# Down projection of a hybrid decoder step: three groups of contraction tiles, two of them in seven products for eight

## Chip, core and metric

The kernel runs on one core of a Trainium2 chip. The metric is the device time of one execution in microseconds (us). TensorE (PE) multiplies, VectorE (DVE), ScalarE (ACT) and GpSimd (POOL) do the elementwise work, and SyncE (SP) issues nearly all transfers, in order.

## What is computed

One layer of a decoder trunk, for 512 prompt tokens and 64 sampled tokens (NT = 576 columns), width 1024, everything in float32. Only the feed-forward part and what follows it matter here (D_FF = 2816 = 22 tiles of 128, D_MODEL = 8 tiles of 128):

```python
hf = rmsnorm(h, w['norm_ffn'])
h = h + (jax.nn.silu(hf @ w['w_gate']) * (hf @ w['w_up'])) @ w['w_down']
gate = jax.nn.sigmoid(rmsnorm(h, w['norm_ple']) @ w['w_ple_gate'])
h = h + gate * (p.astype(h.dtype) @ w['w_ple_proj'])
return rmsnorm(h, norm_final)
```

## The kernel before

**Layout.** Activations are held transposed: a tile is 128 features by 576 tokens. A matmul takes a 128x128 block of weights and 288 columns, one of two column halves, `N1` and `N2`. To keep float32 precision, every operand is split into a high part and a remainder (`split` L185, `wsplit` L197): ACT copies the high part, DVE or POOL subtracts it from the source to get the low part, and three matmuls (high by high, high by low, low by high) make one product. Which of DVE and POOL subtracts alternates from split to split (`flip`, L192 and L204) unless the call names one.

**Plain products.** `linear` (L225) loads weights in blocks of four contraction tiles (`wload`, a 128x512 block of 256 KB, three `raw` buffers), splits each, and issues 3 x 4 x 2 matmuls per block.

**The seven-product form.** `gate_pair` (L1411) makes two output tiles of the gate projection. It treats the 8 contraction tiles as two halves of four, the two output tiles as the rows, and the two column halves as the columns of a 2x2 block product, which it does in seven products instead of eight (Winograd's form of Strassen's scheme). It loads four weight blocks a11, a21, a22 (three buffers, tag `raw2`) and a12 (tag `raw`, shared with `wload`), and forms s1 = a21 + a22, s2 = s1 - a11, s4 = a12 - s2 on DVE and a11 - a21 on POOL (L1416 to L1419). Each of the seven `product` calls (L1399) splits its weight combination (tags `wh`, `wl`, three buffers each; three of the low parts are named for POOL, four for DVE) and issues 12 matmuls. `kept` (L1406) copies four of the sums out of PSUM on ACT, POOL adds three of them (L1429, L1434, L1435), and DVE finishes the two outputs and scales them by `rs`, the row norms. The right-hand combinations of the normed input, T1 to T4, are built once, at L1377 to L1387.

**The feed-forward stage.** Pair 0 is done plainly (L1355). For pairs 1 to 10, `gate_pair` is followed by two plain up projections (`linear(XF, ...)`, L1460, 96 matmuls), their product with silu(gate), and `inner` (L1350), which splits the two finished inner tiles into `ah`, `al` (low part on POOL). `down` (L1446) is called after pair 5 with 12 inner tiles and after pair 10 with 10: for each of 8 output tiles it runs `linear`, scales the sum by `rs` on DVE (L1451) and adds it to the residual tile `hs[c]` on POOL (L1452). The second call also runs `after` (L1299) for each output tile: ACT makes the high part and a square, DVE the low part (L1303), POOL adds up the squares (L1310). The gate of the per-layer embedding (L1498 on) takes these as its operands; the weights of its second and third output tile wait for the root of the norm (L1499), its first does not.

**Order of the work.** A planner orders the instructions of each engine when the program is built: in program order, with later instructions drawn forward where its timing model sees an engine idle. Each engine's order is then fixed, and its instructions wait for their inputs in that order. PSUM is used in four tiles of two banks (`lin_bank`, L103).

Of the kernel before, what the change touches and what calls it, by code (L numbers as in the profile page):

```python
# [16 lines left out]
P = 128  # L17
D = 1024
NT = 576
# [1 line left out]
HALF = 288  # L21
KT = D // P
NFF = 22
NSPLIT = 6
C_DECAY = math.exp(-0.5)
EPS = 1e-6
GN_EPS = 64e-5
# [48 lines left out]
def hybrid_step(ctx, tc, A):  # L76
# [1271 lines left out]
    AF2 = []  # L1348

    def inner(s_):  # L1350

# [3 lines left out]
    for f in range(2):  # L1355
        ps = lin_ps()
        linear(XF, ps, WLAST)
        if f == 0:
            up = lin_ps()
            linear(XF, up, WLAST)  # L1360
            rs = rstd_of(st)
        s_ = ft("sg")
        V.tensor_tensor(s_[:], ps, rs[:], ALU.mult)
        act(s_[:], s_[:], AF.Silu)
        if f:
            up = lin_ps()
# [29 lines left out]
        wat[0] += P * 512  # L1396
        return t

    def product(ps, w, n, first, eng):  # L1399
        hi, lo = split(w[:], cm, ("wh", "wl"), [P, 512], lo_eng=eng, bufs=3)  # L1400
        for p, q in WLAST:
            for k in range(4):
                T.matmul(ps, (hi, lo)[p][:, k * P:(k + 1) * P], OPS[n][k][q], start=first and p == q == k == 0,  # L1403
                         stop=p == 1 and k == 3, skip_group_check=True)

    def kept(ps):  # L1406
# [1 line left out]
        act(t[:], ps)  # L1408
        return t

    def gate_pair():  # L1411

        a11, a21, a22 = (block() for _ in range(3))
        a12 = block(wp, "raw")
        s1, s2, s4 = (cm.tile([P, 512], F32, tag="sw", name=nm("sw"), bufs=3) for _ in range(3))
        V.tensor_tensor(s1[:], a21[:], a22[:], ALU.add)  # L1416
        V.tensor_tensor(s2[:], s1[:], a11[:], ALU.subtract)
        G.tensor_tensor(a21[:], a11[:], a21[:], ALU.subtract)
# [4 lines left out]
        product(a, a11, "B11", True, V)  # L1423
        p1 = kept(a)
        product(b, s2, "T2", True, G)
        p6 = kept(b)
        product(c, s1, "T1", True, V)
        p5 = kept(c)
        G.tensor_tensor(p6[:], p6[:], p1[:], ALU.add)  # L1429
        product(a, a12, "B21", False, G)  # L1430
        V.tensor_tensor(sa[:, N1], a, rs[:, N1], ALU.mult)
        product(b, a21, "T3", False, V)
# [3 lines left out]
        product(c, s4, "B22", False, G)  # L1436
        V.tensor_tensor(sa[:, N2], c, p6[:], ALU.add)
        V.tensor_tensor(sa[:, N2], sa[:, N2], rs[:, N2], ALU.mult)
        product(b, a22, "T4", False, V)
        V.tensor_tensor(sb[:, N1], b, p1[:], ALU.add)  # L1440
        V.tensor_tensor(sb[:], sb[:], rs[:], ALU.mult)
        for s_ in (sa, sb):
            act(s_[:], s_[:], AF.Silu)
        return sa, sb

    def down(last):  # L1446
        for c in range(8):
            ps = lin_ps()
            linear(AF2, ps, WLAST)
            t = ft("dn")  # L1450
            V.tensor_tensor(t[:], ps, rs[:], ALU.mult)  # L1451
            G.tensor_tensor(hs[c][:], hs[c][:], t[:], ALU.add)  # L1452
            if last:
                after(c, hs[c], "norm_ple", pools[-1], "f", 9, st)
        AF2.clear()

    for p in range(1, NFF // 2):
        for s_ in gate_pair():
            up = lin_ps()
            linear(XF, up, WLAST)  # L1460
            V.tensor_tensor(s_[:], up, s_[:], ALU.mult)
            inner(s_)
# [72 lines left out]
def pack(inp):  # L1535
# [79 lines left out]
    for c in range(0, NFF, 2):  # L1615
# [7 lines left out]
        if c // 2 in (NSPLIT - 1, NFF // 2 - 1):  # L1623
            k0 = 0 if c // 2 == NSPLIT - 1 else 2 * NSPLIT
            for m in range(8):
                put_tile(wd, k0, c + 2 - k0, m)
    for c in range(8):
        put_tile(wpg, 0, 8, c)
    out["wts"] = np.concatenate(blocks)
# [43 lines left out]
```

## Time and profile before

| what | value |
|---|---|
| median of 3 runs | 1347.17 us (1346.14 to 1347.79) |
| span of the profiled execution, first to last instruction | 1349.0 us; its own device time is not listed beside the span, so the span stands for it |
| PE busy | 1246.8 us (92% of the span), 10525 matmuls |
| DVE, ACT, POOL busy | 826.0, 618.9, 625.6 us |
| transfers | 135.58 MB, mean 100 GB/s |
| feed-forward stage | about 862 to 1280 us of the span |

In the profile, "busy" is the time in which an engine has an instruction under way. Matmuls are pipelined, so the mean length of one (about 295 ns) is more than the distance from one to the next. A row such as `wl<-sw,wh` names what is written, then what is read. Times on the left of the timeline are microseconds from the start of the span.

### The profile page before, as it was taken

The page shows a single profiled execution, that of the slowest core. Times are in us where ns is not written, and L with a number is a line of the kernel's source. Part 1 is how long each engine was busy: PE and PEld are TensorE (multiplying, and loading weights), DVE is VectorE, ACT ScalarE, POOL GpSimd, SP SyncE. Part 2 cuts the span into 40 slices and gives each one's busy share as a digit, 9 for nine tenths or more (in the row PEclk, how much of TensorE's full clock was granted, in tenths as well). Part 3 has the DMA queues.
Part 4 walks back from the last instruction along what each step waited for, and adds up shares of the span by engine and source line. Part 5 has one row for each costly group of instructions (what it writes and reads, how often), then busy time and mean ns, then how long its engine had stood idle before and what let it go on. Part 6 is the DMA issues. An engine that isn't in the chain of part 4 may idle for free.

```text
span 1349.0 us, 26596 instructions
## 1 busy us (share of the span) xinstructions
PE 1246.8 (92%) x10525; PEld 1150.7 (85%) x10525; DVE 826.0 (61%) x1443; ACT 618.9 (46%) x1256; POOL 625.6 (46%) x597
## 2 busy tenths in 40 slices
PE   6897999999989978899999969989999999999997
PEld 6787897889868957788779859889999999999997
DVE  6648666887687785943466667886553135443454
ACT  6565436534654463343434364464442124433363
POOL 5425413642355154122456645565654336654642
PEclk9897799899979978889989989998999999999998
DMA  5322242234232412262454542222323222314322
GB/s 164 125 68 66 77 117 63 85 103 116 75 99 78 109 41 80 94 214 83 157 176 131 179 125 72 73 93 88 92 88 87 79 86 82 93 59 149 96 89 71
DMA packets 94461, 135.58 MB, mean 100 GB/s; under 512 B 34705, under 2 KB 39057, under 8 KB 94337
## 3 DMA queue, kind: packets, MB, share of 16 engines
q1 hardware_dynamic: 93760, 133.36, 32.4%
q8 instruction: 83, 1.36, 0.4%
q10 hardware_dynamic: 576, 0.52, 0.1%
q14 instruction: 42, 0.34, 0.1%
HBM read 106.10 MB, written 27.75 MB: 99 GB/s over the span
## 4 chain that ended last, share of the span: by engine, by line
PE 63%; DVE 14%; ACT 4%; issue 4%; DMA 3%; POOL 3%; DVEq 0%; SPq 0%; ACTq 0%; POOLq 0%
PE lin L234 21%; PE lin L1403 8%; PE lin L223 6%; PE lin L221 6%; PE lin L222 6%; DVE h L395 2%; PE lin L1508 1%; PE lin L1509 1%; PE lin L1510 1%; DVE tmp L674 1%; DVE wlo L206 1%; DVE Tt L676 1%; PE lin L613 1%; PE cx L797 1%; DVE suv L831 1%
## 5 line engine op out<-in xcount | busy, mean ns | idle before, releaser
L206 POOL TENSOR_TENSOR wlo<-raw,whi 128x512 fp32r<-128x512 f32 (+1 forms) x108 | 146.4, 1356 | 352.5 <-ACT whi L93 269.5
L93 ACT ACTIVATE whi<-raw 128x512 fp32r<-128x512 f32 (+1 forms) x232 | 143.3, 618 | 259.1 <-PE lin L234 126.4
L221 PE MATMUL lin<-xhi,whi 128*128 128x288 f32 (+1 forms) x784 | 243.3, 311 | 2.5 <-ACT whi L93 2.2
L223 PE MATMUL lin<-xhi,wlo 128*128 128x288 f32 (+1 forms) x784 | 241.5, 308 | 2.3 <-POOL wlo L206 2.3
L222 PE MATMUL lin<-xlo,whi 128*128 128x288 f32 (+1 forms) x784 | 241.5, 308 | 0.3 <-POOL xlo L194 0.3
L206 DVE TENSOR_TENSOR wlo<-raw,whi 128x512 fp32r<-128x512 f32 (+1 forms) x124 | 100.9, 814 | 103.2 <-PE lin L234 60.4
L221 PEld LDWEIGHTS lin<-xhi,whi 128*128 128x128 f32 (+1 forms) x784 | 151.0, 193 | 9.3 <-ACT whi L93 2.6
L223 PEld LDWEIGHTS lin<-xhi,wlo 128*128 128x128 f32 (+1 forms) x784 | 150.7, 192 | 6.2 <-POOL wlo L206 2.8
L222 PEld LDWEIGHTS lin<-xlo,whi 128*128 128x128 f32 (+1 forms) x784 | 150.8, 192 | 4.8 <-issue 1.2
L234 PE MATMUL lin<-xhi,whi 128*128 128x288 f32 x384 | 62.3, 297 | 3.2 <-ACT xhi L93 3.0
L234 PE MATMUL lin<-xlo,whi 128*128 128x288 f32 x384 | 60.8, 298 | 0.0
L234 PE MATMUL lin<-xhi,wlo 128*128 128x288 f32 x384 | 59.3, 297 | 0.0
L234 PEld LDWEIGHTS lin<-xhi,whi 128*128 128x128 f32 x384 | 54.6, 189 | 3.8 <-ACT xhi L93 1.7
L234 PEld LDWEIGHTS lin<-xlo,whi 128*128 128x128 f32 x384 | 54.8, 191 | 0.0
L234 PE MATMUL lin<-ah,wlo 128*128 128x288 f32 x352 | 54.7, 296 | 0.0
L234 PE MATMUL lin<-al,whi 128*128 128x288 f32 x352 | 54.7, 296 | 0.0
L234 PE MATMUL lin<-ah,whi 128*128 128x288 f32 x352 | 54.7, 296 | 0.0
L234 PEld LDWEIGHTS lin<-xhi,wlo 128*128 128x128 f32 x384 | 54.3, 191 | 0.0
L1403 PE MATMUL lin<-T,wh 128*128 128x288 f32 x320 | 50.1, 296 | 4.5 <-DVE T L194 2.8
L674 DVE TENSOR_TENSOR tmp<-L,Tt 72x30 f32<-72x30 f32 (+14 forms) x120 | 49.2, 410 | 3.2
L234 PEld LDWEIGHTS lin<-ah,whi 128*128 128x128 f32 x352 | 49.6, 189 | 0.0
L234 PEld LDWEIGHTS lin<-ah,wlo 128*128 128x128 f32 x352 | 49.6, 189 | 0.0
(425 smaller groups left out, 3197.8 us busy)
## 6 DMA issues: line engine op xcount, KB each, us to landing
raw<-wts SPq DMA_DIRECT2D x271, 256.0 KB, 2.6
S<-s_wkv SPq DMA_DIRECT2D x8, 512.0 KB, 5.1
hd<-s_ssm SPq DMA_DIRECT2D x8, 512.0 KB, 4.5
o_ssm_s<-hd SPq DMA_DIRECT2D x8, 512.0 KB, 2.9
xbc_d<-E SPq DMA_DIRECT2D x12, 288.0 KB, 2.1
x<-xT SPq DMA_DIRECT2D x8, 288.0 KB
gate_d<-g SPq DMA_DIRECT2D x8, 288.0 KB, 2.5
bv_d<-rw SPq DMA_DIRECT2D x8, 288.0 KB
```

Source lines behind the costliest of these rows:

```text
L93: return S.activation(out, in_, func, bias=bias, scale=scale)
L206: eng.tensor_tensor(lo[:, 0:n], raw[:, 0:n], hi[:, 0:n].bitcast(F32), ALU.subtract)
L221: T.matmul(ps[:, a:b], whi, xhi[:, a:b], start=first, stop=False)
L222: T.matmul(ps[:, a:b], whi, xlo[:, a:b], start=False, stop=False)
L223: T.matmul(ps[:, a:b], wlo, xhi[:, a:b], start=False, stop=last)
L234: T.matmul(ps[:, a:e], (hi, lo)[p][:, i * P:(i + 1) * P], xs[k + i][q][:, a:e], start=n == k + i == 0, stop=n == 2 and k + i == nk - 1, sk ...
L395: V.scalar_tensor_tensor(h[:], E[:, i:i + 600], w(i), h[:], ALU.mult, ALU.add)
L613: T.matmul(ps[:, c:c + 128].rearrange("p (a t) -> p a t", a=2), s.BK[jj][H[e], g].rearrange("p a t -> p (a t)"), s.G[H[e], g, jj, :, e], s ...
L674: V.tensor_tensor(o, L[:, jx:jx + 1, jx + 1:32].to_broadcast([NB, jx, n]), Tt[:, 0:jx, jx:jx + 1].to_broadcast([NB, jx, n]), ALU.mult)
L676: V.tensor_tensor(Tt[:, 0:jx, jx + 1:32], Tt[:, 0:jx, jx + 1:32], o, ALU.subtract)
L797: T.matmul(uw[H[e], jj, :], TT[H[e], g, jj, :], xs[H[e], jj, :], start=True, stop=True)
L1403: T.matmul(ps, (hi, lo)[p][:, k * P:(k + 1) * P], OPS[n][k][q], start=first and p == q == k == 0, stop=p == 1 and k == 3, skip_group_check ...
```

## The change

The 22 inner tiles are cut into three groups: pairs 0 to 3, pairs 4 to 7 and pairs 8 to 10 (`DOWNS = (4, 8)`). The first two groups of 8 inner tiles go through the seven-product form, for two output tiles at a time; the last group of 6 stays plain.

- `gate_pair`'s body becomes `seven(ops, r)`, with the operands and an optional scale as arguments. Without a scale, ACT copies the first quarter of the output out of PSUM and the two DVE multiplications by `rs` fall away.
- `operands(sa, sb)` replaces `inner` for pairs 0 to 7: four subtractions over half the columns (three on DVE, one on POOL) build the right-hand combinations, and four splits (one of 288 columns, three of 576) replace two. The split of B11 lies in buffers of tag `hx`, four of them, which take the place of the residual tiles 4 to 7.
- `down_pairs(d)` runs `seven` four times, for output tiles 0-1 to 6-7, and stores each of the eight sums, unscaled, to DRAM (`acc_d`).
- The residual tiles `hs[4]` to `hs[7]` are stored to DRAM when they are complete (`h_d`) and loaded again after the last pair.
- The last group: for each output tile two stored sums are loaded and added on POOL, DVE adds the plain product of the last 6 inner tiles and multiplies by `rs`, POOL adds the residual, then `after` as before. The pool of the late stage has 12 instead of 9 working tiles.
- The host packs the weights of the down projection in the new order.

```diff
-NSPLIT = 6
+DOWNS = (4, 8)
...
+    h_d, acc_d = dram("h", 4), [dram(f"acc{i}", 8) for i in range(2)]
...
     def residual(c, ps, src):
-        h = hp.tile([P, NT], F32, tag="h", name=nm("h"))
+        h = hp.tile([P, NT], F32, tag="hx" if c > 3 else "h", name=nm("h"), bufs=4)
...
         after(c, hs[c], "norm_ffn", me, "xs", 8, st)
+        if c > 3:
+            nc.sync.dma_start(h_d[c - 4][:], hs[c][:])
...
-        return pools[-1].tile([P, NT], F32, tag="f", name=nm(name), bufs=9 if len(pools) > 1 else 6)
+        return pools[-1].tile([P, NT], F32, tag="f", name=nm(name), bufs=12 if len(pools) > 1 else 6)
...
-    def product(ps, w, n, first, eng):
+    def product(ps, w, x, first, eng):
...
-                T.matmul(ps, (hi, lo)[p][:, k * P:(k + 1) * P], OPS[n][k][q], start=first and p == q == k == 0,
+                T.matmul(ps, (hi, lo)[p][:, k * P:(k + 1) * P], x[k][q], start=first and p == q == k == 0,
...
-    def gate_pair():
+    def seven(ops, r=None):
...
-        V.tensor_tensor(sa[:, N1], a, rs[:, N1], ALU.mult)
+        if r is None:
+            act(sa[:, N1], a)
+        else:
+            V.tensor_tensor(sa[:, N1], a, r[:, N1], ALU.mult)
...
+    def operands(sa, sb):
+
+        i = len(DOPS.setdefault("B11", []))
+        t, u = ft("t12"), ft("t34")
+        V.tensor_tensor(t[:, N1], sa[:, N2], sa[:, N1], ALU.subtract)
+        G.tensor_tensor(u[:, N1], sb[:, N2], sa[:, N2], ALU.subtract)
+        V.tensor_tensor(t[:, N2], sb[:, N2], t[:, N1], ALU.subtract)
+        V.tensor_tensor(u[:, N2], sb[:, N1], t[:, N2], ALU.subtract)
+        b = hp.tile([P, 2, HALF], F32R, tag="hx", name=nm("b11"), bufs=4)
+        hi, lo = split(sa[:, N1], None, None, None, hi=b[:, 0], lo=b[:, 1])
+        DOPS["B11"].append((hi, lo))
+        for n, (x, names) in enumerate(((sb, ("B21", "B22")), (t, ("T1", "T2")), (u, ("T3", "T4")))):
+            f = 3 * i + n
+            hl = split(x[:], fp, (f"ah{f}", f"al{f}"), [P, NT])
+            for c, name in zip((N1, N2), names):
+                DOPS.setdefault(name, []).append(tuple(y[:, c] for y in hl))
+
+    def down_pairs(d):
+        for c in range(0, 8, 2):
+            for i, t in enumerate(seven(DOPS)):
+                nc.sync.dma_start(acc_d[d][c + i][:], t[:])
+        DOPS.clear()
+
+    operands(*held)
     for p in range(1, NFF // 2):
-        for s_ in gate_pair():
+        pair_ = gate_pair()
+        for s_ in pair_:
             up = lin_ps()
             linear(XF, up, WLAST)
             V.tensor_tensor(s_[:], up, s_[:], ALU.mult)
-            inner(s_)
-        if p == NSPLIT - 1:
-            down(False)
+            if p >= DOWNS[-1]:
+                inner(s_)
+        if p < DOWNS[-1]:
+            operands(*pair_)
+        if p + 1 in DOWNS:
+            down_pairs(DOWNS.index(p + 1))
+    for c in range(4, 8):
+        hs[c] = hp.tile([P, NT], F32, tag="hx", name=nm("h"), bufs=4)
+        nc.sync.dma_start(hs[c][:], h_d[c - 4][:])
     cm_.close()
     pools.append(ctx.enter_context(tc.tile_pool(name="f2", bufs=1, side="right", reuse_waits="tile")))
     st = {"x": []}
-    down(True)
+    for c in range(8):
+        old = [ft("acc") for _ in acc_d]
+        for t, src in zip(old, acc_d):
+            nc.sync.dma_start(t[:], src[c][:])
+        G.tensor_tensor(old[0][:], old[0][:], old[1][:], ALU.add)
+        ps = lin_ps()
+        linear(AF2, ps, WLAST)
+        t = old[1]
+        V.tensor_tensor(t[:], ps, old[0][:], ALU.add)
+        V.tensor_tensor(t[:], t[:], rs[:], ALU.mult)
+        G.tensor_tensor(hs[c][:], hs[c][:], t[:], ALU.add)
+        after(c, hs[c], "norm_ple", pools[-1], "f", 12, st)
```

More of the change, by code (lines that the diff above doesn't have):

```diff
@@ L1344, in ft @@
     def ft(name):
[L1345 removed]
+        return pools[-1].tile([P, NT], F32, tag="f", name=nm(name), bufs=12 if len(pools) > 1 else 6)
     XF = st["x"]
[L1348 removed]
+    AF2, held, DOPS = [], [], {}
     def inner(s_):
@@ L1368, in hybrid_step @@
         V.tensor_tensor(s_[:], up, s_[:], ALU.mult)
-        inner(s_)
+        held.append(s_)
     cm_ = ExitStack()
@@ L1435, in gate_pair @@
         G.tensor_tensor(sb[:, N2], p67[:], p5[:], ALU.add)
-        product(c, s4, "B22", False, G)
+        product(c, s4, ops["B22"], False, G)
         V.tensor_tensor(sa[:, N2], c, p6[:], ALU.add)
-        V.tensor_tensor(sa[:, N2], sa[:, N2], rs[:, N2], ALU.mult)
-        product(b, a22, "T4", False, V)
+        if r is not None:
+            V.tensor_tensor(sa[:, N2], sa[:, N2], r[:, N2], ALU.mult)
+        product(b, a22, ops["T4"], False, V)
         V.tensor_tensor(sb[:, N1], b, p1[:], ALU.add)
-        V.tensor_tensor(sb[:], sb[:], rs[:], ALU.mult)
+        if r is not None:
+            V.tensor_tensor(sb[:], sb[:], r[:], ALU.mult)
+        return sa, sb
+    def gate_pair():
+        sa, sb = seven(OPS, rs)
         for s_ in (sa, sb):
@@ L1444, in gate_pair @@
         return sa, sb
[L1446 to L1455, printed above, removed]
+    def operands(sa, sb):
[19 more added lines that the diff above has]
+    operands(*held)
     for p in range(1, NFF // 2):
-        for s_ in gate_pair():
+        pair_ = gate_pair()
+        for s_ in pair_:
             up = lin_ps()
@@ L1622, in pack @@
             put_tile(wu, 0, 8, c + i)
[L1623 to L1626, printed above, removed]
+        if c // 2 + 1 in DOWNS:
+            lo_, hi_ = (list(range(c - 6 + i, c + 2, 2)) for i in range(2))
+            for m in range(0, 8, 2):
+                for ks, i in ((lo_, 0), (lo_, 1), (hi_, 1), (hi_, 0)):
+                    put(wd, ks, m + i)
+    for m in range(8):
+        put_tile(wd, 2 * DOWNS[-1], NFF - 2 * DOWNS[-1], m)
     for c in range(8):
```

11 lines of the change are left out of this document (5 added, 6 removed).

## The prediction

> **What bounds the kernel now.** I read the page first (busy shares, then the chain that ended last), then the feed-forward stage by windows, then the rows of the engines beside PE.
>
> ```profile
> span 1349.0 us, 26596 instructions
> PE 63%; DVE 14%; ACT 4%; issue 4%; DMA 3%; POOL 3%; DVEq 0%; SPq 0%; ACTq 0%; POOLq 0%
> L234 PE MATMUL lin<-ah,wlo 128*128 128x288 f32 x352 | 54.7, 296 | 0.0
> raw<-wts SPq DMA_DIRECT2D x271, 256.0 KB, 2.6
> ```
>
> PE is 63% of the chain. The third row is one of the three forms of the down projection: 3 x 352 = 1056 matmuls. The windows show the stage that the change touches: PE, PEld, DVE, ACT and POOL busy, then granted clock, DMA share and GB/s.
>
> ```profile
> 886.00:911.00 25.00, 20.74 (x153) 19.98 (x151) 24.41 (x30) 18.23 (x37) 19.51 (x16) 0.99 0.22 68
> ...
> 1020.00:1096.00 76.00, 76.00 (x572) 76.00 (x571) 15.97 (x21) 15.83 (x26) 29.67 (x21) 1.00 0.28 80
> 1101.74:1197.30 95.56, 95.56 (x723) 95.56 (x722) 53.07 (x64) 42.36 (x76) 58.39 (x44) 1.00 0.30 86
> 1217.00:1280.00 63.00, 63.00 (x474) 63.00 (x474) 21.82 (x28) 23.41 (x39) 35.61 (x26) 1.00 0.37 115
> ```
>
> The second row is the first call of the down projection, the third is four pairs of gate and up, the fourth the last call. PE is never idle in any of them, at full clock, so a matmul taken away there is worth its distance to the next: 76.00/572 = 0.133 us. The first row is where T1 to T4 are built: DVE and POOL are busy for 24.41 and 19.51 of 25.00 us, and PE falls to 20.74. So PE is the bound by a margin that the other engines can use up.
>
> **What is removed.** Two groups of four `seven` calls have 2 x 4 x 84 = 672 matmuls, the last group 8 x 6 x 6 = 288: 960 for 1056. 96 x 0.133 = **-12.7 us**, all on the path.
>
> **What the seven products ask of DVE and POOL.** The rows give shortest, median and longest.
>
> ```profile
> L194 DVE TENSOR_TENSOR wl<-raw,wh x14: 679/683/1470, 1100.3 to 1204.6; 128x512 fp32r<-128x512 f32 x14
> ...
> L1416 DVE TENSOR_TENSOR sw<-raw,raw x9: 692/852/1295, 923.5 to 1184.2; 128x512 f32<-128x512 f32 x9
> ...
> L194 POOL TENSOR_TENSOR wl<-sw,wh x9: 1286/1297/1746, 1103.6 to 1199.6; 128x512 fp32r<-128x512 f32 x9
> ...
> L194 POOL TENSOR_TENSOR al<-sb,ah x4: 1432/1442/1448, 1124.0 to 1196.2; 128x576 fp32r<-128x576 f32 x4
> ...
> L1418 POOL TENSOR_TENSOR raw<-raw,raw x9: 1292/1299/1793, 924.6 to 1184.9; 128x512 f32<-128x512 f32 x9
> ...
> L1429 POOL TENSOR_TENSOR e<-e,e x5: 804/813/1262, 1104.8 to 1200.8; 128x288 f32<-128x288 f32 x5
> ```
>
> Why the same operation takes 0.68 or 1.47 us, the timeline shows:
>
> ```profile
> 1163.79 1.88 POOL L194 TENSOR_TENSOR al<-sa,ah 128x576 fp32r<-128x576 f32 x1
> ...
> 1164.38 1.83 DVE L206 TENSOR_TENSOR wlo<-raw,whi 128x512 fp32r<-128x512 f32 x1
> 1166.14 0.45 DVE L1440 TENSOR_TENSOR sb<-lin,e 128x288 f32<-128x288 f32 x1
> ```
>
> The two operations fill 1163.79 to 1166.21, 2.42 us; the POOL one takes 1.43 undisturbed (the row of al above) and the DVE one's 0.68, together 2.11. They ran one after the other. DVE operations that read PSUM keep their 0.45.
>
> [...]
>
> Per `seven`, at shortest durations: DVE 3 combinations x 0.69 + 4 low parts x 0.68 = 4.8 (its two PSUM adds left out); POOL 1 combination x 1.29 + 3 low parts x 1.29 + 3 additions x 0.81 = 7.6; one after the other 12.4 us, while its 84 matmuls take 84 x 0.133 = 11.2. The same count for a present pair of gate and up, which has the same seven products and 96 more matmuls to hide them: DVE 7.4 (two more low parts, two scalings), POOL 13.0 (two more low parts, two of 576 columns), 20.4 us in 23.9, and PE has no idle time. So the seven products cost nothing at 85% and must show at 111%. **Bounds** per `seven`: 0 if the two engines overlap a little more than the pair did; at most 12.4 - 11.2 = 1.2 for the sharing plus 0.9 for the handover worked out next. I take 1.2, because the crowded first window is nearest (PE lost 4.3 of 25.00 us, 17%, which would be 1.9 of 11.2, part of it start-up): 8 x 1.2 = **+9.6 us** (0 to 17).
>
> The handover from one `seven` to the next: the third block's buffer is free when its low part is made, and then come the transfer, s1, s2 and ACT:
>
> ```profile
> 1157.60 0.33 SPq L1395 DMA_DIRECT2D raw<-wts  x1
> 1160.35 0.88 DVE L1416 TENSOR_TENSOR sw<-raw,raw 128x512 f32<-128x512 f32 x1 [0.82 <-DMA raw<-wts]
> ...
> 1161.83 1.33 DVE L1417 TENSOR_TENSOR sw<-sw,raw 128x512 f32<-128x512 f32 x1
> ...
> 1163.19 0.63 ACT L93 ACTIVATE wh<-sw 128x512 fp32r<-128x512 f32 x1 [0.57 <-DVE sw L1417]
> ```
>
> At best 2.75 + 0.88 + 1.33 + 0.63 = 5.6 us. With three `wh` buffers the seventh split starts when the fourth product ends; its ACT and DVE parts take 0.63 + 0.9, so the second product of the next `seven` has its weights 7.2 us after the fourth product, and PE gets there in 4 x 12 x 0.133 = 6.4. It is 0.9 short, unless the planner puts a product that needs no sum ahead. Today 96 up matmuls (12.8 us) lie between. The stores of the sums go into SP's queue and wait for the `seven`'s last adds; weight loads behind them wait too. I price that at nothing, as the loads of the next `seven` wait for buffers freed earlier; without that cover it is a landing of 2.6 us, within the upper bound.
>
> **Entry into each group.** T2 needs the last inner tile: in the trace its product (0.76), the ACT split (0.69); a subtraction of 288 columns (0.45, the PSUM row above) now lies between, and the low part follows.
>
> ```profile
> 1169.95 0.76 DVE L1461 TENSOR_TENSOR sb<-lin,sb 128x576 f32<-128x576 f32 x1 [0.75 <-ACT sb L93]
> ...
> 1170.74 0.69 ACT L93 ACTIVATE ah<-sb 128x576 fp32r<-128x576 f32 x1 [0.30 <-DVE sb L1461]
> ```
>
> 1.9 us with their gaps, of which the first product hides 1.6, before anything queued on DVE: 0.3 to 2 per group, I take 1.0: **+2.0 us**. Before, 12 inner tiles per output hid it.
>
> **Operands for pairs 1 to 7.** POOL loses two low parts (2 x 1.43) and DVE and POOL share 3 x 0.45 + 0.81 and four low parts, about 3.9: the serial sum of a pair goes from 20.4 to 23.6 of 23.9 us. That is 99%, between the two cases above. 0 to 1.1 us a pair; I take 0.2: **+1.4 us**. Pair 0's operands fall into the crowded window, 3 x 0.45 and two low parts, about 3 us, more of DVE where PE waited 4.3; PE has up products to draw forward: 0 to 3, I take **+0.5**.
>
> **The last group.** Each output tile has 36 matmuls, 4.8 us, where it had 60. POOL has for each: the new addition of the two stored sums, the residual, the square (six of eight), and the low part of one 512-column block. (Which engine gets it follows from the number of splits ahead of it: 204 for 156, an even difference, so the first block of each output tile stays with POOL.)
>
> ```profile
> L1452 POOL TENSOR_TENSOR h<-h,dn x16: 1428/1621/1816, 1030.6 to 1281.2; 128x576 f32<-128x576 f32 x16
> ...
> L1310 POOL TENSOR_TENSOR hsq<-hsq,hsq x6: 1431/1690/1827, 1236.5 to 1276.8; 128x576 f32<-128x576 f32 x6
> ```
>
> At shortest: 16 x 1.43 + 6 x 1.43 + 7 x 1.29 + 1.43 (last inner tile) + 1.29 (first weights of the next stage) = 43.2; with the medians 46.2. PE needs 288 x 0.133 = 38.3. So POOL becomes the bound, unless it adds the stored sums early: 12 working tiles let four of eight go ahead, 5.7 us. How the end hangs on POOL today:
>
> ```profile
> 1279.62 0.70 PE L234 MATMUL lin<-ah,wlo 128*128 128x288 f32 x4
> ...
> 1280.36 0.76 DVE L1451 TENSOR_TENSOR dn<-lin,rstd 128x576 f32<-128x576 f32 x1 [0.76 <-PE lin L234]
> ...
> 1281.19 1.44 POOL L1452 TENSOR_TENSOR h<-h,dn 128x576 f32<-128x576 f32 x1 [2.82 <-DVE dn L1451]
> ...
> 1282.67 0.78 ACT L93 ACTIVATE xhi<-h,pv 128x576 fp32r<-128x576 f32 x1 [5.20 <-POOL h L1452]
> ...
> 1284.01 0.41 PE L1508 MATMUL lin<-xhi,wp 128*128 128x320 f32 x1
> ```
>
> The residual is complete 2.3 us after PE's last down matmul, and PE fills the time with the first matmuls of the next stage, which need only the earlier tiles. Now there is one more DVE operation (0.8), and POOL's queue behind it: 0.8 at least, 46.2 + 2.5 (its start, behind the last pair) - 38.3 - 2.3 = 8.1 at most; I take the middle, **+4.0 us**.
>
> The other transfers (4 + 16 stores and as many loads of 288 KB, 11.8 MB on 135.58) fit a DMA share of 0.28 to 0.37: nothing. The four stores of the residual tiles stand in SP's queue behind their additions, with the next weight blocks behind them, for which there are three buffers: nothing.
>
> **Sum:** -12.7 + 9.6 + 2.0 + 1.4 + 0.5 + 4.0 = +4.8 us on the profiled span of 1349.0. The median of the runs is 1347.2, 1.8 below the span; the same difference gives **1352.0 us**.
>
> **The rivals.** *Faster.* PE stays the bound throughout: the planner draws sum-free products forward at the handovers and prepares the first `seven` of each group during the up products. For it: not a us of PE idle time in 95.56 with the same seven products. Against: 111% for 85%. The price is then 0.25 per `seven`, 1 for the entries, 0.5 and 1 at both ends: -12.7 + 4.5 = -8.2, 1339.0. It decides below 0.6 us per `seven`. *No change.* Half of each: `seven` at 0.8, POOL's end at 2.5: -12.7 + 6.4 + 2 + 0.7 + 0.5 + 2.5 = -0.6, 1346.6. *Full exclusion.* DVE and POOL take strict turns and the handover adds to it, 2.1 per `seven`, and POOL's end costs 8.1: -12.7 + 16.8 + 2 + 1.4 + 0.5 + 8.1 = +16.1, 1363. [...] Against it: in the first window the two engines' busy time adds up to 43.92 in 25.00, and PE still ran 83%. That the products are not fewer can be ruled out from the loop bounds.
>
> **Numbers.** A measurement of this kernel tells about 0.2%, 2.7 us, from no change. Forecast 0.42, faster rival 0.28, no change 0.17, full exclusion 0.13. Low end 1337 (half of the faster rival and its bound), high end 1361. The forecast's own range is 1349.9 to 1357. Slower is 0.42 + 0.13.
>
> **What would show it.** Matmuls of the down projection 960; PE below 95% in the two group stretches, with waits on `wl` (DVE or POOL), on `sw` and on T; POOL at over 85% there and DVE low parts at over 1 us mean; POOL without a gap through the last group and its residual addition as the releaser of the next stage. If PE stands at 100% in the groups, the 9.6 is wrong; if the last residual comes within 3.5 us of the last down matmul, the 4.0 is.

## The result, and the profile after

| what | before | after |
|---|---|---|
| median | 1346.84 us (1346.14 to 1347.79) | 1392.11 us (1384.84 to 1395.52, 4 runs) |
| ratio | | 1.0353, 95% interval 1.0325 to 1.0381 |
| span of the profiled execution | 1349.0 us | 1391.1 us (its own time 1393.14) |

The change makes the kernel 45 us slower. The forecast was 1352.0, its range 1337 to 1361. The direction was right, the size was not: the measured time lies 31 us above the top of the range. The page of the changed kernel, in the lines that answer to those of before:

```profile
span 1391.1 us, 26794 instructions
PE 55%; DVE 21%; ACT 6%; issue 5%; DMA 5%; POOL 4%; SPq 0%; DVEq 0%; ACTq 0%; POOLq 0%
```

PE's share of the chain falls from 63% to 55%, DVE's rises from 14% to 21%. The windows say where. Their columns are the stretch, its length, then PE, PEld, DVE, ACT and POOL busy with their instructions, granted clock, DMA share, GB/s. The boundaries are the starts of the DVE product of up and silu(gate) for the second tile of pairs 3, 4, 7, 8 and 10, and then the reciprocal that belongs to the root of the norm (DVE, `rn<-rn`), called the root below; pairs 4 and 7 are rounded to 1055.00 and 1127.00 for 1054.73 and 1126.99. Before, from pair 3 to pair 10, then to the root, and the whole from pair 0:

```profile
974.11:1217.02 242.91, 242.91 (x1831) 242.91 (x1830) 103.47 (x127) 87.70 (x154) 127.90 (x95) 1.00 0.29 86
1217.02:1285.72 68.70, 68.57 (x539) 67.92 (x537) 23.38 (x30) 26.43 (x45) 37.05 (x27) 1.00 0.35 109
897.19:1285.72 388.53, 383.66 (x2883) 382.05 (x2881) 178.01 (x222) 150.84 (x269) 214.34 (x160) 0.99 0.30 89
```

After, a pair with a group, three pairs, a pair with a group, two pairs, the last group, and the whole from pair 0:

```profile
974.66:1055.00 80.34, 72.83 (x518) 70.45 (x517) 49.42 (x58) 35.98 (x71) 53.80 (x41) 0.98 0.37 112
1055.00:1127.00 72.00, 72.00 (x545) 72.00 (x544) 56.30 (x64) 34.16 (x62) 47.34 (x35) 1.00 0.29 85
1127.00:1207.26 80.26, 71.89 (x520) 69.28 (x519) 50.73 (x57) 36.03 (x71) 55.49 (x41) 1.00 0.41 127
1207.26:1254.07 46.81, 46.81 (x355) 46.81 (x354) 20.15 (x28) 19.53 (x36) 26.52 (x21) 1.00 0.25 77
1254.07:1327.49 73.42, 49.16 (x349) 46.13 (x347) 24.47 (x34) 21.22 (x37) 44.43 (x31) 0.83 0.42 138
895.88:1327.49 431.61, 384.29 (x2792) 374.59 (x2791) 271.42 (x318) 185.53 (x349) 280.70 (x209) 0.96 0.34 105
```

Read the last rows of both fences first. There are 91 matmul records fewer (96 by the loops, and a few are missing), yet PE is busy as long as before, 384.29 for 383.66 us, and idle for 47.32 instead of 4.87. The saving was made, and was eaten twice: by idle time and by a longer busy time per matmul. (The last section says how the two hang together.)

From pair 3 to pair 10 the kernel before took 242.91 us. The change adds 96 matmuls there (672 for 576), 12.7 us at the old distance, so 255.6; it took 279.4, that is **+23.8** for the two groups. From pair 10 to the root there are 192 matmuls fewer, 25.5 us, so 43.2; it took 73.4, **+30.2** for the last group. Pairs 0 to 3 took 78.8 for 76.9, **+1.9**. The head up to pair 0 is 1.3 shorter, the end after the root 0.3 longer. -12.7 + 23.8 + 30.2 + 1.9 - 1.3 + 0.3 = 42.2; the spans differ by 42.1.

**The last group.** The waits from pair 10 to the root (engine, line, what it waited for: total, times, longest), and POOL's timeline there:

```profile
ACT xhi L93 <- POOL h L1510: 36.2, 8, 6.4
PE lin L1551 <- ACT xhi L93: 16.5, 4, 5.9
DVE acc L1508 <- POOL acc L1504: 16.2, 7, 2.7
POOL hsq L1311 <- ACT hsq L93: 9.0, 6, 1.5
POOL h L1510 <- DVE acc L1509: 9.0, 6, 1.7
```

```profile
1300.94 1.43 POOL L1510 TENSOR_TENSOR h<-h,acc 128x576 f32<-128x576 f32 x1 [1.66 <-DVE acc L1509]
1303.89 1.41 POOL L1311 TENSOR_TENSOR hsq<-hsq,hsq 128x576 f32<-128x576 f32 x1 [1.52 <-ACT hsq L93]
1305.25 1.40 POOL L1504 TENSOR_TENSOR acc<-acc,acc 128x576 f32<-128x576 f32 x1
1308.32 1.40 POOL L1510 TENSOR_TENSOR h<-h,acc 128x576 f32<-128x576 f32 x1 [1.66 <-DVE acc L1509]
```

This is a loop of 7.4 us from one residual addition to the next (1300.94, 1308.32), closed by POOL's order. The addition of the stored sums of a tile (L1504) needs nothing but two loads, but it stands in POOL's queue behind the previous tile's addition of squares (L1311). That one waits for ACT's square, ACT for POOL's residual addition (L1510), this for DVE's two operations, and these for L1504. POOL sits idle for 1.66 and 1.52 us in every turn, and is busy for 44.43 us of 73.42. The sums of the last four output tiles all lay in PSUM by then: PE's last down matmul ended at 1297.7, the last residual was ready at 1324.4, 26.7 us later, where it had been 2.3.

**The groups.** PE's waits in the first of them, and the timeline around the longest:

```profile
PE lin L1405 <- ACT wh L93: 3.0, 2, 2.3
PE lin L1405 <- ACT e L93: 1.5, 3, 0.5
PE lin L1405 <- ACT ah L93: 1.4, 1, 1.4
PE lin L1405 <- POOL wl L194: 1.0, 1, 1.0
```

```profile
1010.59 1.36 DVE L194 TENSOR_TENSOR wl<-raw,wh 128x512 fp32r<-128x512 f32 x1 [3.32 <-ACT wh L93]
1011.98 0.33 SPq L1397 DMA_DIRECT2D raw<-wts  x1
1014.98 0.69 DVE L1418 TENSOR_TENSOR sw<-raw,raw 128x512 f32<-128x512 f32 x1 [2.07 <-DMA raw<-wts]
1015.71 0.69 DVE L1419 TENSOR_TENSOR sw<-sw,raw 128x512 f32<-128x512 f32 x1
1016.77 0.63 ACT L93 ACTIVATE whi<-raw 128x512 fp32r<-128x512 f32 x1 [3.55 <-DMA raw<-wts]
1017.60 1.14 ACT L93 ACTIVATE wh<-sw 128x512 fp32r<-128x512 f32 x2
1018.27 0.80 PE L1405 MATMUL lin<-ah,wh 128*128 128x288 f32 x4 [2.30 <-ACT wh L93]
```

A block's buffer comes free when its low part is made (1011.95), the next load goes out at once, and the two sums follow as soon as the data is there. The second is ready at 1016.40, but ACT splits it only at 1017.60: another block's split, which waits for a transfer of its own (1016.77), and a copy out of PSUM stand ahead in ACT's order. PE gets its weights 6.3 us after the buffer came free. This is the handover of the prediction, one in-order wait longer; 1.2 of PE's 2.3 us are ACT's delay.

PE is idle for 7.5 us in the first group and 8.4 in the second. The waits sort into three kinds. Weights of the next product (`wh`, `wl`): 4.0 and 4.4 us. The last operand at the entry (`ah`): 1.4 and 1.8. ACT's copies that empty PSUM (`e`, `sa`): 2.1 and 2.2.

### The profile page after: what moved, and what is told of

Read it like the earlier page. It is cut to its first block, busy times and chain, and to the rows that moved or that the text cites. A ratio compares the mean times of both kernels' runs of the same rounds, so it can differ in the third digit from the quotient of the medians.

```text
span 1391.1 us, 26794 instructions
## 1 busy us (share of the span) xinstructions
PE 1241.5 (89%) x10429; PEld 1135.9 (82%) x10429; DVE 917.6 (66%) x1539; ACT 653.3 (47%) x1336; POOL 691.2 (50%) x645
## 4 chain that ended last, share of the span: by engine, by line
PE 55%; DVE 21%; ACT 6%; issue 5%; DMA 5%; POOL 4%; SPq 0%; DVEq 0%; ACTq 0%; POOLq 0%
PE lin L234 11%; PE lin L1405 11%; PE lin L221 6%; PE lin L223 6%; PE lin L222 6%; DVE h L396 2%; DVE wlo L206 2%; DMA raw<-wts 2%; DVE tmp L675 1%; DVE Tt L677 1%; PE lin L1551 1%; PE lin L1552 1%; PE lin L1553 1%; DVE suv L832 1%; PE lin L614 1%
## 5 line engine op out<-in xcount | busy, mean ns | idle before, releaser
L206 POOL TENSOR_TENSOR wlo<-raw,whi 128x512 fp32r<-128x512 f32 (+1 forms) x92 | 128.9, 1401 | 306.4 <-ACT whi L93 237.2
L93 ACT ACTIVATE whi<-raw 128x512 fp32r<-128x512 f32 (+1 forms) x200 | 122.9, 615 | 176.8 <-PE lin L222 73.0
L221 PEld LDWEIGHTS lin<-xhi,whi 128*128 128x128 f32 (+1 forms) x784 | 148.9, 190 | 10.4 <-ACT whi L93 2.6
L206 DVE TENSOR_TENSOR wlo<-raw,whi 128x512 fp32r<-128x512 f32 (+1 forms) x108 | 87.4, 810 | 57.1 <-ACT whi L93 36.3
L194 DVE TENSOR_TENSOR wl<-raw,wh 128x512 fp32r<-128x512 f32 x54 | 50.0, 926 | 38.5 <-ACT wh L93 25.4
L93 ACT ACTIVATE wh<-raw 128x512 fp32r<-128x512 f32 x72 | 45.0, 627 | 48.1 <-PE lin L1405 27.3
L194 POOL TENSOR_TENSOR wl<-sw,wh 128x512 fp32r<-128x512 f32 x36 | 54.9, 1525 | 10.6 <-ACT wh L93 7.0
L1551 PE MATMUL lin<-xhi,wp 128*128 128x320 f32 (+1 forms) x128 | 40.3, 315 | 19.1 <-ACT xhi L93 16.5
L1405 PEld LDWEIGHTS lin<-T,wh 128*128 128x128 f32 x320 | 44.9, 188 | 6.6 <-ACT T L93 2.4
```

The lines of the kernel that those rows point to most:

```text
L93: return S.activation(out, in_, func, bias=bias, scale=scale)
L194: eng.tensor_tensor(lo[:], src, hi[:].bitcast(F32), ALU.subtract)
L206: eng.tensor_tensor(lo[:, 0:n], raw[:, 0:n], hi[:, 0:n].bitcast(F32), ALU.subtract)
L221: T.matmul(ps[:, a:b], whi, xhi[:, a:b], start=first, stop=False)
L1405: T.matmul(ps, (hi, lo)[p][:, k * P:(k + 1) * P], x[k][q], start=first and p == q == k == 0, stop=p == 1 and k == 3, skip_group_check=True)
L1551: T.matmul(ps, hi, xh, start=k == 0, stop=False)
```

## The experiments

Theory: the last group lost its time to the order of POOL's queue, not to the amount of POOL's work; the groups lost theirs to the handover of weight blocks from one `seven` to the next. Rivals: POOL's work in the last group, and DVE and POOL taking turns in the groups. "Tail" is the stretch from pair 10 to the root (73.4 us), "a pair with a group" that from pair 3 to 4 and from 7 to 8 (80.1 and 80.3 from start to start; at the old distances a pair's 95.56 / 4 = 23.9 and 336 x 0.133 for the group make 68.6, where the expectations write 68.7). Stretches are read from one profile per kernel. Where a run left them untouched they came out at 79.1 to 80.3 (a pair with a group) and 72.4 to 73.4 (the tail), so differences below about 1 us say little. The start of pair 3 lies anywhere from 967.0 to 975.4 us, so whole times carry what happens ahead of it too. Ratios are to the kernel before, run beside each kernel. The names in brackets are those that the expectations use.

### Stored sums added two tiles ahead (adds_ahead)

```diff
+    old_sum(0)
+    old_sum(1)
     for c in range(8):
-        old = [ft("acc") for _ in acc_d]
-        for t, src in zip(old, acc_d):
-            nc.sync.dma_start(t[:], src[c][:])
-        G.tensor_tensor(old[0][:], old[0][:], old[1][:], ALU.add)
+        if c < 6:
+            old_sum(c + 2)
+        old = olds[c]
```

> Undoes the order alone in the last group: the loads and POOL additions of the stored sums stand two output tiles ahead in the program, so that on POOL they no longer stand behind the square of the tile before. POOL's work is the same. If the order is the cause (a loop of about 7.4 us per tile through POOL, DVE, POOL, ACT and POOL again), the stretch from the last up product to the root's reciprocal falls from 73.4 us to 46 to 52 and the time from 1392 to 1365 to 1372. If the amount of POOL's work is the cause, as the prediction had it, the stretch stays above 69 and the time above 1388.

Measured: 1374.25 us (1371.04 to 1376.52), ratio to the kernel before 1.0208 (1.0166 to 1.0250). The window of the tail and PE's waits there:

```profile
1248.77:1305.35 56.58, 47.34 (x349) 45.55 (x347) 35.69 (x35) 21.45 (x37) 49.08 (x31) 0.94 0.54 179
```

```profile
PE lin L234 <- POOL wlo L206: 5.3, 3, 3.4
PE lin L1563 <- POOL wp L206: 3.3, 1, 3.3
```

The tail of 56.6 us and the time lie between the two forecasts. The same operations in another order bring 16.8 us: the order theory holds for that much. (The loads of the sums go out earlier as well, but POOL's waits for them fall only from 4.6 to 3.3 us.) It doesn't hold for all. POOL is now busy for 49.08 of 56.58 us and makes the low parts of weights too late for PE: 8.6 of PE's 9.2 us of idle time. Its 31 operations take 4.65 us longer than in the loop (44.43). So the rival, POOL's work, has a part in the remaining 13 us, one that only shows once the order is mended; fold, below, takes 11.2 us of them.

### Stored sums added on DVE (adds_dve)

```diff
-        G.tensor_tensor(old[0][:], old[0][:], old[1][:], ALU.add)
...
-        V.tensor_tensor(t[:], ps, old[0][:], ALU.add)
+        V.tensor_tensor(t[:], ps, t[:], ALU.add)
+        V.tensor_tensor(t[:], t[:], old[0][:], ALU.add)
```

> In the last group DVE adds both stored sums, POOL none: 8 x 1.4 us less work on POOL, one more DVE operation of 0.76 us in each tile's chain, and no POOL operation ahead of the DVE additions. Order theory: the loop is gone too, the stretch falls to 44 to 50 us, time 1363 to 1370. Work theory: it falls by what POOL loses, about 11 us, to 62, time about 1381.

Measured: 1376.5 us (1372.93 to 1385.43), ratio 1.0235 (1.0171 to 1.0299), tail 64.0. The numbers are near the work theory's 62 and 1381, the trace is not: POOL is busy for only 33.18 us of the tail. DVE in the tail:

```profile
1299.86 0.82 DVE L1304 SCALAR_TENSOR_TENSOR xlo<-h,pv,xhi 128x576 fp32r<-128x576 f32 x1 [2.32 <-ACT xhi L93]
1300.60 0.75 DVE L1507 TENSOR_TENSOR acc<-lin,acc 128x576 f32<-128x576 f32 x1
1301.38 1.18 DVE L1508 TENSOR_TENSOR acc<-acc,acc 128x576 f32<-128x576 f32 x1
1302.59 0.76 DVE L1509 TENSOR_TENSOR acc<-acc,rstd 128x576 f32<-128x576 f32 x1
1305.67 0.82 DVE L1304 SCALAR_TENSOR_TENSOR xlo<-h,pv,xhi 128x576 fp32r<-128x576 f32 x1 [2.32 <-ACT xhi L93]
```

The loop has moved to DVE's queue, 5.8 us a turn: the next tile's product (L1507) stands behind this tile's low part (L1304), which waits for ACT, ACT for POOL's residual addition, and that for L1509. Taking 11 us of work off POOL brought 9.4 us and no more, because each step still stood behind the one before it.

### Four buffers for two of a seven's blocks (room)

All eight residual tiles go to DRAM, and their four slots hold blocks a11 and a21 of the down sevens.

```diff
-        a11, a21, a22 = (block() for _ in range(3))
+        a11, a21, a22 = (block(*((hp, "h") if r is None and i < 2 else ())) for i in range(3))
```

> In the two groups of seven products the first and second weight block of each call get four buffers of their own (the residual tiles 0 to 3 are stored and reloaded like 4 to 7), so that the loads of the next call no longer wait for the low parts of this one. Work on DVE and POOL is the same. Each group now takes 56 us beyond a pair of gate and up, for 44.7 us of matmuls. If the handover through the weight buffers is the main cause, a group falls to 47 to 51 us. If the amount of work on DVE and POOL, taking turns, is the cause, it stays at 54 to 57.

Measured: 1373.16 us (one run). A pair with a group, both times:

```profile
967.03:1041.03 74.00, 70.74 (x520) 69.16 (x519) 48.85 (x55) 35.70 (x71) 51.70 (x40) 1.00 0.39 122
1113.19:1189.15 75.96, 72.29 (x528) 70.25 (x527) 48.27 (x54) 36.06 (x71) 52.59 (x40) 1.00 0.43 136
```

80.1 and 80.3 became 74.0 and 76.0: room alone gives back 10.4 of the 23.8 us, with the same operations on every engine. PE's idle time falls by 4.2 and 4.7 us, and its waits for ACT's `wh` from 3.0 and 1.9 us to none and 0.6. Less a pair, the groups take 50.1 and 52.1 us: the first as the handover theory said (47 to 51), the second 1 us over. (The span is 19.7 us shorter in all; 7.6 of the rest lie ahead of pair 3, before the first down seven, and no run shows why.)

### POOL's additions left out (no_pool_adds)

```diff
-        G.tensor_tensor(p6[:], p6[:], p1[:], ALU.add)
+        if r is not None:
+            G.tensor_tensor(p6[:], p6[:], p1[:], ALU.add)
```

and the other two likewise, with ACT copying the quarter straight into its tile; part of the down projection is left out.

> In the two groups of seven products the three POOL additions of each call are left out (of the sums that complete the second and fourth quarter; ACT copies one of them instead), 2.4 to 3.5 us of POOL's 9 per call. If DVE and POOL taking turns is the cause, each group falls from 56 us by 6 to 11. If the handover through the weight buffers is, it falls by less than 3.

Measured: 1382.56 us (one run). A pair with a group:

```profile
971.67:1047.94 76.27, 70.92 (x514) 68.54 (x513) 48.58 (x57) 35.93 (x71) 43.80 (x30) 1.00 0.37 115
1120.51:1198.86 78.35, 72.89 (x520) 70.75 (x519) 46.73 (x57) 36.32 (x72) 44.86 (x30) 0.98 0.41 130
```

80.1 and 80.3 fall by 3.8 and 1.9 us, although POOL's busy time falls by 10 and 10.6. That is less than the 6 to 11 that turns would give; the second is inside the handover's forecast (less than 3), the first is above it. So the additions cost something here. PE waits less for weights (`wh` and `wl`: 1.2 and 0.9 us for 4.0 and 4.4), which turns and a delayed handover would both show, so this run doesn't tell them apart.

### The stored sums folded into the residual early (fold)

During pairs 9 and 10 DVE adds two stored sums, scales them and adds them to the residual tile; the last group is then as in the kernel before.

```diff
+            V.tensor_tensor(a[:], a[:], b[:], ALU.add)
+            V.tensor_tensor(a[:], a[:], rs[:], ALU.mult)
+            V.tensor_tensor(hs[c][:], hs[c][:], a[:], ALU.add)
...
-        V.tensor_tensor(t[:], ps, old[0][:], ALU.add)
-        V.tensor_tensor(t[:], t[:], rs[:], ALU.mult)
+        V.tensor_tensor(t[:], ps, rs[:], ALU.mult)
```

> The sevens stay as they are; only the last group changes. The stored sums are added, scaled by rs and put into the residual tiles while the pairs p = 9 and 10 run (three DVE operations of about 0.76 us per output tile, 24 in all, and 20 loads), so that the last group has per tile only what the kernel before had: one DVE product, one POOL addition, and the norm. Theory 'order, then POOL's additions': with adds_ahead the stretch from pair 10 to the root was 56.6 us and POOL without a gap; eight additions of 1.40 less on POOL are 11.2, so 44 to 48 here (PE's own share makes 43.2), and 1362 to 1368 us in all. Rival 'the chain of one tile': if what counts is the chain from the product through POOL h, ACT, DVE and POOL hsq (5.8 us a tile in adds_dve), the stretch stays above 53 us. Rival 'it moves to the pairs': the two pairs up to 10, 46.8 to 47.1 us in the runs so far, grow by more than 4 us.

Measured: 1369.45 us (1368.8 to 1375.75), ratio 1.019 (1.0161 to 1.0218). The windows from pair 7 to 8, from 8 to 10, and the tail:

```profile
1122.16:1215.68 93.52, 79.48 (x548) 76.05 (x547) 73.25 (x80) 37.86 (x74) 60.38 (x43) 0.96 0.51 165
1215.68:1258.79 43.11, 43.11 (x327) 43.11 (x326) 18.61 (x28) 17.50 (x32) 25.14 (x19) 1.00 0.23 71
1258.79:1304.20 45.41, 43.62 (x349) 42.57 (x347) 20.89 (x27) 21.02 (x37) 34.72 (x23) 1.00 0.39 119
```

The tail falls to 45.4, as the order theory with POOL's additions said: 28.0 of the 30.2 us go with the stored sums out of the tail. The whole misses its 1362 to 1368, because the stretch with the second group takes 93.5 us for 80.3 (the two pairs after it take 43.1 for 46.8, net 9.5). The planner had drawn the fold forward into the second group, which was already the tightest place: DVE has 80 operations there instead of 57, and PE's waits for DVE rise from 1.5 to 7.1 us.

### Ups between the sevens (interleave, and both with the fold)

```diff
-        pair_ = gate_pair()
+        pair_, nxt = nxt or gate_pair(), None
+        todo and next(todo)
         for i, s_ in enumerate(pair_):
...
+            todo and next(todo)
```

`next(todo)` issues one `seven` of the group; the sums take the slots of residual tiles 0 to 3.

> The last group stays as it is (73 us). Each group's four sevens stand apart: gate products of the next pair, seven, up, seven, up, seven, gate products of the pair after it, seven. The number of operations on every engine is the same. Theory 'handover': a seven loses time because its seven products follow one another faster than the weight blocks, their sums and low parts come through three buffers each, and at the entry because PE has nothing else to do while the last operands are made; between up products both are covered. From pair 3 to pair 5 (and 7 to 9) it took 105.3 and 105.0 us, where the matmuls alone make 92.7; it should take 94 to 98, and the whole 1372 to 1380 us. Theory 'DVE and POOL in turns': the work and the clashes are as many as before, so 101 to 105 and 1385 to 1392 us.

Measured: 1384.11 us (1379.45 to 1386.91), ratio 1.0285 (1.0256 to 1.0313). Pairs 3 to 5 and 7 to 9 took 100.5 and 98.6 us, between the two forecasts, as the whole is. Taken to the next pair after the group, 3 to 6 and 7 to 10, it is 126.0 and 122.9 for 128.3 and 127.1: 2.3 and 4.2 us. Spreading the sevens is worth less (6.5 us) than giving them room (10.4). With the fold added:

> Both edits together, fold and interleave. If the two causes are separate and both theories hold, the savings add up: 1392 less 26 less 12 to 20, that is 1346 to 1354 us, about the time of the kernel before; PE's 12.7 us saved would then be left over by what remains in the groups. If the interleaved pairs have no room for the fold (DVE also carries the operands there), 1356 to 1364.

Measured: 1367.09 us (1364.3 to 1371.71), ratio 1.0161 (1.0127 to 1.0196). The tail is 46.1, but pair 7 to 10 takes 134.0 us for 122.9, the fold drawn forward again: outside both forecasts.

### The fold held back, with room (room_fold)

```diff
+        with tc.issue_after(last[0].ins):
+            if s:
+                fold(*F[s - 1])
+            if s < len(F):
+                fetch(*F[s])
```

What stands under `issue_after` can't be placed ahead of the instruction named, here the up product of the half pair.

> The fold as before, but each part of it is held until the up product of its half pair is out, so that the planner can't draw it forward into the end of the second group, and two of a seven's four blocks have four buffers of their own (as in room). In fold, the stretch from pair 7 to pair 8 was 93.5 us instead of 80.3 while the two pairs after it were 43.1 instead of 46.8: the fold's DVE work had been drawn into the end of the group, net loss about 9.5 us. Theory: held back it hides in the pairs, so that 9.5 us come back, and the room gives back 5 us a group as it did alone: 1369 less 9.5 less 10, that is 1347 to 1354 us, with the tail still 45 to 48 and the stretches with a group 74 to 76. Rival: DVE and the transfers have no room in the pairs either, and pairs 8 to 10 get longer by what the group gains: 1356 to 1362.

Measured: 1353.63 us (1351.7 to 1359.42), ratio 1.009 (1.0061 to 1.0118). Pair 7 to 8, 8 to 10 and the tail:

```profile
1115.60:1192.65 77.05, 74.56 (x547) 72.76 (x546) 48.34 (x54) 37.41 (x73) 54.42 (x41) 1.00 0.55 180
1192.65:1243.74 51.09, 47.96 (x349) 47.55 (x348) 45.08 (x49) 18.05 (x34) 29.86 (x21) 0.97 0.30 83
1243.74:1288.77 45.03, 42.38 (x336) 40.85 (x334) 24.33 (x28) 20.89 (x37) 35.28 (x23) 1.00 0.42 133
```

The theory's 1347 to 1354 just holds. The group is back at 77.0 (73.3 the first), and the fold now costs 4.3 us in the two pairs (51.1 for 46.8), as the rival had it, if by less. DVE is full there, 45.08 of 51.09, and PE's one wait, 3.1 us, is for DVE.

### No two down sevens in a row (ups_between)

The order is gate, up, seven, up, seven, gate, up, seven, up, seven; the operands of both pairs are made after the last seven, and the fold's addition into the residual is on POOL.

> The sevens of a group in the order gate, up, seven, up, seven, gate, up, seven, up, seven: no two down sevens in a row, and one ordinary half pair (gate, up) between the last operands and the first down seven. In interleave, with gate, seven, up, seven, up, seven, gate, seven, two pairs with a group took 100.5 us instead of 105.3 (matmuls 92.7), and PE's waits lay where two or three sevens stood in a row and where the first seven met ACT still busy with the operands. Theory 'handover and entry': what is left is where D and a gate seven meet, so two pairs with a group take 95 to 98 us, and with the fold held back and on POOL in its last part the whole 1344 to 1352 us. Rival 'the work itself': still 100 us, and 1354 to 1362.

Measured: 1359.52 us (1358.8 to 1360.94), ratio 1.012 (1.0098 to 1.0143). The first group and the second:

```profile
970.00:1070.00 100.00, 94.82 (x689) 92.97 (x688) 66.19 (x78) 45.05 (x89) 64.38 (x49) 0.98 0.35 106
1120.79:1220.00 99.21, 97.79 (x730) 96.85 (x729) 64.27 (x72) 47.05 (x91) 68.36 (x52) 1.00 0.46 152
```

In the second group PE is idle for 1.4 of 99 us, so sevens can be fed nearly without loss. In the first it is idle for 5.2 of 100, of which 3.5 are one wait for DVE to empty a PSUM bank, and pair 3 to 6 takes 128.6 as with the change (128.3). Why the two differ isn't shown; the operands of pair 4 had been drawn into the first. Pair 7 to 10 takes 130.8, where interleave took 122.9: the fold lies in it, and PE is idle for another 7.8 us after 1220. The whole lies where the rival had it, and is no better than room_fold.

### The addition on POOL, and no additions in the sevens (fold_pool, no_adds)

```diff
-            V.tensor_tensor(hs[c][:], hs[c][:], a[:], ALU.add)
+            G.tensor_tensor(hs[c][:], hs[c][:], a[:], ALU.add)
```

> As room_fold, with the addition into the residual on POOL instead of DVE and one tile per half pair from pair 8 on. In room_fold PE was busy 42.87 of 46 us in the stretch 1190 to 1236 while DVE had 42.07: the fold's 24 DVE operations had filled it. Theory 'what is left is idle time of PE wherever DVE is full': those 3 us come back and the whole stands 2 to 4 us lower than room_fold, 1349 to 1352 us where the kernel before has 1342 to 1347. Rival: POOL's 1.4 us additions delay the low parts of the weights that POOL makes, and it stays at 1353 to 1358.

Measured: 1353.66 us (1348.48 to 1356.76, 10 runs), ratio 1.0063 (1.0039 to 1.0087). Pairs 8 to 10 took 51.7 us for 51.1: the 3 us didn't come back, as the rival said. With room_fold, whose interval overlaps, it is the best version that was run, and still 0.6% slower than the kernel before. Its two groups hold 14.6 us more than their matmuls and a pair, the pairs 8 to 10 3.9, the tail 1.9: 20.4 us against the 12.7 saved.

> As the kernel above, but POOL's three additions in each seven of the groups are left out (ACT copies one quarter instead), so part of the down projection is missing. With room, a pair with a group takes 74 to 76 us where the matmuls make 68.7 (two pairs' worth of gate and up included). If the rest is DVE and POOL delaying each other, the stretches fall to 69 to 71 us; if it is the entry and the evacuation of the banks through ACT, they stay at 73 to 75.

Measured: 1354.67 us (one run). A pair with a group, first with POOL's additions, then without:

```profile
970.92:1044.93 74.01, 70.79 (x521) 69.20 (x520) 48.32 (x55) 35.59 (x71) 51.63 (x40) 1.00 0.38 122
```

```profile
971.52:1044.89 73.37, 70.91 (x521) 69.26 (x520) 42.52 (x55) 36.47 (x71) 40.11 (x29) 1.00 0.39 120
```

0.6 us less in the first group, 1.4 in the second (76.5 for 77.8), with 11.5 us less POOL work. Of the forecasts for turns (69 to 71) and for entry and evacuation (73 to 75) the first group meets the second; the second group lies above both. And room_fold, with the additions, had 73.3 and 77.0, so this is within what two runs differ by. Once the blocks have room, the additions cost next to nothing. That what they cost without room came by delaying the handover is the likeliest reading; no run separates it from turns. Against 68.6 us (one pair and the group, not two pairs) there remain 4.8 in the first group, of which 2.5 are idle time of PE; entry and evacuation through ACT are the candidates, and no run separates them.

## Why the prediction was wrong

- **Removed matmuls, -12.7:** right in the count (91 records fewer, a few missing), but PE's busy time didn't fall, because each matmul was busy longer on average (384.29 us for 2792 records, 383.66 for 2883).
- **Operands, +1.9 in all:** right in size. Pairs 0 to 3 took 1.9 longer, where the forecast had 1.1 of its 1.9; pair 4 to 7 took 72.3 us for 3 x 23.9, another 0.6, with PE never idle in 1055 to 1127. The equal total is chance.
- **The last group, +4.0 (0.8 to 8.1):** the step that failed most. Measured 30.2. It counted POOL's operations, took POOL as gap-free, and gave the work as the bound (43.2 to 46.2 us). The work term was not far off: with the sums added ahead POOL was busy for 49.1 us. (The medians of its own rows make 47.8, not 46.2, and the middle of 0.8 and 8.1 is 4.5, not 4.0; neither matters beside 30.2.) What the sum left out was the order: I had allowed that POOL "adds the stored sums early", four of eight tiles ahead, and never asked where these additions stand in its queue. Program order put each addition behind the previous tile's squares, which closed a loop of 7.4 us through POOL, DVE, POOL and ACT, for an output tile that costs PE 4.8. Adding ahead gave 16.8 back, taking the stored sums out of the tail 28.0.
- **Per seven, 8 x 1.2, and the entries, 2.0 (together 11.6):** measured 23.8 with the rest of the pairs (23.1 in the two stretches with a group), twice as much and above the upper bounds together (17 and 4). With the last group at its upper bound of 8.1 this alone would still have left the time above 1361. The forecast chose the sharing of DVE and POOL as the price and left the handover (0.9; its own figures make 5.6 + 0.63 + 0.9 = 7.1, 0.7 over 6.4) to the upper bound. No run shows that sharing at 1.2 us a `seven`: it was my estimate from shortest durations and one pair of operations. The runs showed rather the other way round: room for two blocks gave back 10.4 us; leaving out POOL's additions gave 5.7 without room, and with it 2.0, no more than two runs differ by. The working of the handover had the right chain, but let ACT be free when the sum was ready; in the wait shown above ACT stood in a wait for a transfer. The entries cost 1.4 and 1.8 us of idle time, for 1.0 each. ACT's copies out of PSUM, which made PE wait for 2.1 and 2.2 us, had no term at all. Of the 23.8 us the runs tie 10.4 to the handover; the cause of the rest stays open.
- **What would show it:** PE was below 95% in the groups (91% and 90%), as said, and DVE's 23 low parts of weights averaged 1.03 and 1.12 us there, over 1 us as said. But in four pairs of the kernel before, where PE was never idle, they averaged 0.97, so that sign hardly tells the two apart. POOL was not over 85% (67% and 69%), nor without a gap in the last group, and the last residual came 26.7 us after the last down matmul. So POOL was not full in either place. That doesn't refute the sharing in the groups by itself, where DVE's and POOL's busy time add up to 103.2 of 80.34 us; what speaks against it as the main price is room, which changed none of that work.
- **The rivals:** full exclusion (1363) had the largest prices and was still 29 us short, as it too summed up work. No run shows that the two engines take strict turns. What the traces show is POOL's operations longer where POOL is crowded (the tail's 31 operations in 49.08 us with adds_ahead instead of 44.43 with the change), but that is a second cost; the first, in the last group, was an engine that waited.

## What to carry over

When an engine's work per step nears the bound, write down not only its sum but its order: which instruction of the next step stands behind which wait of this one. The loop through three in-order queues cost the sum of its links per step, 7.4 us, even though no engine in it was full (from 1300.94 to 1323.01 POOL was busy for 12.51 of 22.07 us, DVE for 7.00, ACT for 4.04); work that depends on nothing in the loop belongs ahead of it or out of the stage. A scheme that saves matmuls by more elementwise work and more weight combinations can also need more buffers where its calls follow one another directly (10.4 us here), and idle slots elsewhere don't help if the planner draws the moved work into the tightest place.

## What the runs showed of the hardware

After some stalls PE's matmuls ran at half the clock (granted 0.50). In the loop of the last group (PE, timeline), the same 128x320 matmul, and three windows (PE first, the granted clock third from the end):

```profile
1301.90 0.31 PE L1553 MATMUL lin<-xhi,wp 128*128 128x320 f32 x1
1303.23 0.41 PE L1551 MATMUL lin<-xhi,wp 128*128 128x320 f32 x1 [1.02 <-ACT xhi L93]
...
1310.58 0.64 PE L1551 MATMUL lin<-xhi,wp 128*128 128x320 f32 x1 [5.93 <-ACT xhi L93]
```

```profile
1302.30:1305.00 2.70, 0.97 (x3) 0.48 (x3) 0.82 (x1) 1.35 (x2) 1.18 (x2) 1.00 1.03 372
1310.50:1312.50 2.00, 1.54 (x3) 0.79 (x3) 0.82 (x1) 0.60 (x2) 1.26 (x1) 0.50 0.00 0
1019.30:1022.50 3.20, 3.20 (x16) 3.20 (x15) 1.73 (x3) 1.26 (x2) 2.86 (x2) 0.50 0.70 246
```

Two effects add up. The matmul at 1303.23, which started after a wait of 1.02 us, is listed longer than the one at 1301.90, 0.41 for 0.31, both at a granted 1.00 (in the kernel before, one that starts right behind 128x1 matmuls, with no wait listed, also has 0.41 at 1.00: 1284.01). At a granted 0.50, after a wait of 5.93 us, it takes 0.64 (1310.58). In the loop the clock read 0.98 from 1304.60 to 1306.00 and 0.50 from 1306.00 to 1310.40, while PE was idle. In the first group, after the wait of 2.30 us that ended at 1018.27, it still read 1.00 from 1018.60 to 1019.20; from 1019.30 to 1022.50 it was 0.50, and four matmuls took 0.96 us from start to start (1019.61, 1020.57) for 4 x 0.133 = 0.53. After a wait of 2.54 us that ended at 1300.21 it read 1.00 from 1300.20 to 1302.30. So the length of the wait just before doesn't decide it alone, and what does isn't shown.

The price of the stall before 1018.27 was its 2.30 us and some 1.6 us more (an estimate: half of the 3.20 us), which the forecast's sums in us of idle time left out. In the tail the granted clock is 0.83, and the 349 records fill 49.16 us (0.141 each) where the kernel before had 0.127: some 4.8 us of busy time from both effects. How much of it made the tail longer isn't shown, as the loop set the pace there.
